# Traced durations in the plan of a list scheduler: the matmul costs, the score products and the lag of a DMA landing

## The chip, the cores and the metric

The kernel runs on one core of a Trainium2 chip, as one program. The metric is the device time of one execution in microseconds; a smaller one is better. A core has TensorE (PE), VectorE (DVE), ScalarE (ACT), GpSimd (POOL) and SyncE (SP), each with a queue of its own that it works off in order; SP's queue issues all DMA transfers here.

## The reference

A decoder trunk of two layers on x (1 × 256 × 1024, float32), conditioned by a vector c. Each layer is a SwiGLU FFN at half weight, a token mixer, and a second SwiGLU FFN at half weight. The mixer of layer 0 is stick-breaking attention (16 heads of 64), that of layer 1 a Griffin RG-LRU block (1280 channels). Before every sub-layer stands an RMSNorm with scale and shift, and behind it a gate; shift, scale and gate come from c.

```python
def sublayer_input(x, g, mod_j):
    shift, scale, gate = mod_j[:, 0], mod_j[:, 1], mod_j[:, 2]
    h = rmsnorm(x, g) * (1 + scale[:, None, :]) + shift[:, None, :]
    return h, (1 + gate)[:, None, :]

for layer in range(DEPTH):
    mod = (c_act @ mod_w[layer] + mod_b[layer]).reshape(B, N_SUB, 3, D_MODEL)
    h, g = sublayer_input(x, norm_g[layer, 0], mod[:, 0])
    x = x + MACARON_W * g * swiglu(h, ffn_w_gu[layer, 0], ffn_w_down[layer, 0])
    h, g = sublayer_input(x, norm_g[layer, 1], mod[:, 1])
    ...  # y: attention (layer 0) or RG-LRU (layer 1) of h
    x = x + g * y
    h, g = sublayer_input(x, norm_g[layer, 2], mod[:, 2])
    x = x + MACARON_W * g * swiglu(h, ffn_w_gu[layer, 1], ffn_w_down[layer, 1])
return rmsnorm(x, final_norm_g)
```

The feed-forward width is 2816. All weights are float32, some 250 MB with the 2 × 9216 × 1024 modulation matrix, and each is read once.

## The kernel before

**Data.** x stays on the chip, transposed: eight tiles x[d] of 128 channels by 256 tokens. A product in float32 accuracy is made of three faster ones: each weight tile of 128 × 2048 (1 MB, a ring `raw` of three) is split by ScalarE into a high half `wh` (L497) and by VectorE into the rest `wl` (L500), 1024 columns at a time, in rings of seven each. Activations are split in the same way. One group (`Acc.group`, L526) is three matmuls on one PSUM bank: wh·xh, wh·xl, wl·xh, each of 256 columns. `group32` (L543) is one matmul in four passes.

**Stages, in order of time.** FFN(0,0), attention(0,1), FFN(0,2), FFN(1,0), RG-LRU(1,1), FFN(1,2), and a last norm. An FFN goes over 22 up tiles (`up`, then `swiglu_tile`) and 11 down tiles of 256 rows (`down`). Attention goes over eight pairs of heads (called heads 0 to 7 here): projection, `scores` (masked start, 12 products at L912, softplus on ScalarE, L923 and the split L740 on VectorE), `sums` (running sums, exponent, split), `values` (L959, then the split L967); the projection of V goes in four parts between them, and the last stage is `down` with the eight tiles of `wo`.

**Boundaries.** `down` leaves the last rows of the last two tiles for the end and finishes the column tiles in the order (0,1), (2,3), (4,5), 6, 7. As each is done, `residual` adds it to x[d] (L666), `add_square` adds x[d]² to a running sum (L601), and `scaled` makes from x[d] and the next scale the first inputs of the next stage, with two more columns for the shift (L623 to L626, so 258 columns). `up_first` lets TensorE work on the first two weight tiles with these inputs that are not normalised yet. Between the two it forms the sum over partitions (`rstd`, L608), and the result is multiplied by rstd afterwards. For the other weight tiles `norm_chunk` (L634 to L636) makes normalised inputs.

**Modulation.** Shift, scale and gate of a sub-layer are 24 multiplies of a 128 × 1024 tile with silu(c), each with its sum: `mod_tile`, a load of 512 KB into a ring `rawm` of three, and one VectorE instruction with an accumulator (L564). Eight of them and one `mod_final` (L568 to L585; the shift's is L577) make one vector. The first two vectors are made at the start; the other 16 wait in a list, `todo`, in the order

```python
    parts = [(0, 0, 2), (0, 1, 1), (0, 1, 0), (0, 1, 2), (0, 2, 1), (0, 2, 0), (0, 2, 2)]
    parts += [(1, i, w) for i in range(3) for w in (1, 0, 2)]
```

(layer, sub-layer, 0 shift, 1 scale, 2 gate), and `hook` puts them into the program at some 1.3 to 1.5 for each weight tile. "Multiplies" below are counted over all 144, the first sixteen included; 49 to 64 are the scale and the shift of FFN(0,2).

**What sets the order.** The function `trunk` does not emit instructions. It describes operations to `Program.op`, each with its engine, a cost in ns and what it reads and writes. `Program.schedule` then runs a list schedule over all five engines, and each queue is emitted in the order of the planned starts. An operation of TensorE has a due time, the sum of the costs of the TensorE operations described before it (`nominal`). Going backwards, every other operation gets its due time from its users: their due time less its cost and less a lag (`LAT`) that depends on its engine. At each step an engine takes, of the operations that could start within 60 ns of the first, the one with the earliest due time; VectorE and ScalarE may wait for a more urgent one (`wait_for`). So the planned times of TensorE and of the landings decide which work VectorE, ScalarE and SP put first, and in places the order of TensorE. The planned times have no part in the execution: there, queues and semaphores alone hold.

Costs in the plan: a VectorE instruction 68 + 1.042 n ns, a ScalarE one 93 + 0.83 n, a DMA by its bytes; the matmuls' cost and the lags are the lines that change. The load of a `mod_tile` waits in the plan for the last TensorE operation described before it (`after=[pr.last_pe]`).

Of the kernel before, what the change touches and what calls it, by code (L numbers as in the profile page):

```python
# [15 lines left out]
T = 256  # L16
# [81 lines left out]
                 "start", "end", "seq", "soft", "lat")  # L98


LAT = {"PE": 230.0, "ACT": 210.0, "DVE": 170.0, "DMA": 2000.0, "POOL": 200.0}
START = {"PE": 1170.0, "DVE": 2840.0, "ACT": 1960.0, "DMA": 1750.0}
SAME = {"PE": 0.0, "ACT": 140.0, "DVE": 60.0, "DMA": 0.0, "POOL": 100.0}

# [1 line left out]
class Program:  # L106
# [53 lines left out]
    def lag(a, b, data):  # L160
        if a.eng == b.eng:
            return SAME[a.eng] if data else 0.0
        return (a.lat or LAT[a.eng]) if data else 100.0

    def schedule(self):
# [30 lines left out]
        for o in ops:  # L196
            o.left, o.ready = len(o.deps), 0.0
        free = {e: START.get(e, 0.0) for e in LAT}
        cand = {e: [] for e in LAT}
        for o in ops:  # L200
# [153 lines left out]


def c_mm(n, passes=3):
    return passes * (max(n, 256) / 2.4 + 2.5)


def c_dma(n):  # L360
# [4 lines left out]
def trunk(ctx, tc, xT, cb, par, modw, gu0, gu, wdn, qk, wv, wo, win, wri, wout, out):  # L365
# [3 lines left out]
    pr = Program()  # L369
# [104 lines left out]
    def A(o, i, f, n, r, w, table=None, psum=False, ptr=0, after=(), **kw):  # L474
        def fn():
            act.activation(o(), i(), f, **{k: (v() if callable(v) else v) for k, v in kw.items()})  # L476
        return pr.op("ACT", c_act(n, psum, ptr), fn, r, w, after, table)

    def V(fn, n, r, w, cost=None, ptr=0):
        return pr.op("DVE", cost or c_dve(n) + 62.0 * ptr, fn, r, w)  # L480
# [26 lines left out]
    class Acc:  # L507
# [6 lines left out]
        def group(self, part, o, w, wc, xs, xc, stop, parts=(None,), passes=(0, 1, 2)):  # L514

            b = self.b
            start = not self.started
            self.started = True
            wh, wl = w
            xh, xl = xs  # L520

            def fn():
                seq = ((wh, xh), (wh, xl), (wl, xh))
                for n, i in enumerate(passes):
                    u, v = seq[i]
                    pe.matmul(o(b()), wc(u()), xc(v()), start=start and n == 0, stop=stop and n == len(passes) - 1,  # L526
                              skip_group_check=True)

            n = xs_n[0]
            rd = [wh, wl] + [(t, q) for t in (xh, xl) for q in parts]  # L530
            if not start:
                rd.append((b, "start"))
            wr = [(b, part)] + ([(b, "start")] if start else [])
            return pr.op("PE", c_mm(n, len(passes)), fn, rd, wr)
# [3 lines left out]
    def group32(acc, part, o, w, wc, x32, xc, n, stop):  # L538

        b = acc.b  # L540
        start = not acc.started
        acc.started = True
        pr.op("PE", c_mm(n, 4), lambda: pe.matmul(o(b()), wc(w()), xc(x32()), start=start, stop=stop, skip_group_check=True),  # L543
              [w, x32] + ([] if start else [(b, "start")]), [(b, part)] + ([(b, "start")] if start else []))
# [58 lines left out]
    def rstd(gen):  # L603
        qs = ssq.pop(gen)
        qs = qs if isinstance(qs, tuple) else (qs,)
        b = Buf(banks)
        for i, q in enumerate(qs):
            pr.op("PE", c_mm(T, 4), lambda i=i, q=q: pe.matmul(b()[:, :T], ones, q(), start=i == 0, stop=i == len(qs) - 1),  # L608
                  [q] + [b] * (i > 0), [b])
        r = Buf(rmsr)  # L610
        o = Buf(rstr)
        A(r, lambda: b()[:, :T], AF.Ln, T, [b], [r], table="lnexp", psum=True, ptr=1, bias=eps_t, scale=1.0 / D)
        A(o, r, AF.Exp, T, [r], [o], table="lnexp", scale=-0.5)
        return o
# [123 lines left out]
    def split(y, a, n):  # L738
        A(y[0], a, AF.Copy, n, [a], [y[0]])
        V(lambda: dve.tensor_tensor(y[1](), a(), f32(y[0]()), ALU.subtract), n, [a, y[0]], [y[1]])  # L740
# [66 lines left out]
    def attention(l, s, nxt, hook):  # L807
# [78 lines left out]
        def hd(ap, e):  # L886
            return ap[:, e * S : (e + 1) * S]

        def scores(f):

            qh, ql = qs.pop(f)
            zs[f] = Buf(banks), Buf(banks)
            u = Buf(F, 6, name=f"u{f}")

            def masked(e):
                b = zs[f][e]

                def fn():
                    diag = b().rearrange("p (e t) -> p e t", e=2)[:, :, :P]
                    pe.matmul(diag, ident, mask.rearrange("p (e t) -> p e t", e=2), start=True, stop=False,  # L900
                              skip_group_check=True)
                pr.op("PE", c_mm(T, 1), fn, [], [b])

            zb = zs[f]

            def products():

                for i, (kc, qc) in enumerate(((slice(T, T + P), slice(0, T)), (slice(T + P, 2 * T), slice(P, T)))):
                    for n, (v, w) in enumerate(((qh, qh), (qh, ql), (ql, qh))):
                        for e in range(2):  # L910
                            rows = slice(e * 64, (e + 1) * 64)
                            pe.matmul(zb[e]()[:, BL[i]], v()[rows, kc], w()[rows, qc], start=False,  # L912
                                      stop=i == 1 and n == 2, skip_group_check=True)

            for e in range(2):
                masked(e)
            pr.op("PE", 2 * c_mm(T), products, [qh, ql], list(zb))
            for e in range(2):
                A(lambda e=e: hd(u(), e), lambda b=zs[f][e]: b()[:, :S], AF.Abs, S, [zs[f][e]], [(u, e)], psum=True)
            A(u, u, AF.Exp, W2, [u], [u], table="lnexp", scale=-1.0)  # L920
            A(u, u, AF.Ln, W2, [u], [u], table="lnexp", bias=1.0)
            for e in range(2):
                V(lambda e=e, b=zs[f][e]: dve.scalar_tensor_tensor(hd(u(), e), b()[:, :S], 0.0, hd(u(), e), ALU.max, ALU.add),  # L923
                  S, [zs[f][e], (u, e)], [(u, e)])
            y = ws_[f] = Buf(R, 6, name=f"sh{f}"), Buf(R, 6, name=f"sl{f}")
            split(y, u, W2)
# [49 lines left out]
        for f in range(8):  # L976
            hook(f)
            q_proj(f)
            if f >= 2:
                values(f - 2)  # L980
            if f in (0, 1, 3, 5):
                v_proj((f + 1) // 2)
            if f >= 1:
                sums(f - 1)
            scores(f)
# [289 lines left out]
```

## Time and profile before

| | |
|---|---|
| runs of the kernel | 997.62, 997.88, 999.67 us; median 997.88 |
| profiled execution | 996.92 us, its span 994.8 us, so 2.1 us lie around the span |
| granted TensorE clock | 0.996 of full speed (mean) |
| TensorE | 976.2 us busy (98%), 8096 instructions |
| VectorE | 799.0 us (80%), 1316 instructions |
| ScalarE | 562.3 us (57%), 902 instructions |
| DMA | 251.24 MB, 253 GB/s over the span |
| weight splits on VectorE (L500) | 328, 390.0 us |
| modulation multiplies (L564) | 144, 174.5 us |

The stages in the trace: FFN(0,0) to about 188 us, attention with `wo` to 321, FFN(0,2) to about 505, FFN(1,0), the RG-LRU block and FFN(1,2) to the end. A row of a group, "L500 DVE TENSOR_TENSOR wl<-raw,wh", gives the line, the engine, the operation and output<-inputs. A duration of one instruction contains a start that overlaps the instruction before it, so two of the same kind can start closer together than a duration. "hx" are inputs of a matmul, "arenar" and "arenaf" the phase's large tiles (split activations, scores), "mf" a finished modulation vector.

### The profile page before, as it was taken

What the parts mean: (1) busy time and instruction counts of PE and PEld (TensorE: products, weight loads), DVE (VectorE), ACT (ScalarE), POOL (GpSimd) and SP (SyncE); (2) the same over time, 40 slices, a digit from 0 to 9 for tenths busy, and PEclk for the clock granted to TensorE, in tenths of its full rate; (3) what the DMA queues carried; (4) which work ended last, traced back from release to release, by engine and by line L of the source; (5) the groups of instructions that cost most, each with busy time, mean ns of one, the idle gap of its engine ahead of it and who ended that gap; (6) DMA issues with size and microseconds to landing.
All of it is one profiled execution on the core that took longest, in us unless ns stands there. A gap on an engine that the chain in (4) does not pass through costs nothing.

```text
span 994.8 us, 19695 instructions
## 1 busy us (share of the span) xinstructions
PE 976.2 (98%) x8096; PEld 964.5 (97%) x8096; DVE 799.0 (80%) x1316; ACT 562.3 (57%) x902; POOL 2.2 (0%) x14
## 2 busy tenths in 40 slices
PE   6999999999999999999999999999999999999997
PEld 5999999999999899999999999999999999999996
DVE  7997888798888999888789988874997996555433
ACT  5475453478785754445366544443779785444333
POOL 0000000000000000000000000000000000000000
PEclk9999999999999999999999999999999999999999
DMA  8988899835556499889866888985244645555431
GB/s 332 352 325 315 331 333 330 334 136 203 198 206 236 170 341 336 331 327 341 326 246 253 329 327 333 343 324 212 108 134 164 254 175 209 204 175 186 166 115 43
DMA packets 48331, 251.24 MB, mean 253 GB/s; under 512 B 5489, under 2 KB 6129, under 8 KB 28530
## 3 DMA queue, kind: packets, MB, share of 16 engines
q1 hardware_dynamic: 48242, 249.99, 68.5%
q8 instruction: 63, 1.03, 0.4%
q14 instruction: 26, 0.21, 0.1%
HBM read 248.92 MB, written 1.05 MB: 251 GB/s over the span
## 4 chain that ended last, share of the span: by engine, by line
PE 95%; DVE 2%; DMA 1%; issue 0%; ACT 0%; SPq 0%; DVEq 0%
PE bank L526 89%; PE bank L836 2%; PE bank L1033 1%; PE bank L959 1%; DVE rawm L564 1%; PE bank L543 1%; PE bank L912 1%; PE bank L937 1%; DMA rawm<-in_modw 1%; DMA x<-in_xT 0%; PE bank L608 0%; PE bank L939 0%; DVE ssq L601 0%; DVE wl L500 0%; DVE x L666 0%
## 5 line engine op out<-in xcount | busy, mean ns | idle before, releaser
L526 PE MATMUL bank<-hx,wh 128*128 128x256 f32 (+1 forms) x3392 | 610.2, 283 | 5.1 <-ACT hx L476 4.8
L526 PEld LDWEIGHTS bank<-hx,wh 128*128 128x128 f32 x3392 | 522.3, 189 | 8.2 <-ACT hx L476 5.7
L497 ACT ACTIVATE wh<-raw 128x1024 fp32r<-128x1024 f32 (+1 forms) x328 | 336.8, 1046 | 340.1 <-PE bank L526 228.6
L500 DVE TENSOR_TENSOR wl<-raw,wh 128x1024 fp32r<-128x1024 f32 (+1 forms) x328 | 390.0, 1210 | 133.2 <-ACT wh L497 130.0
L526 PE MATMUL bank<-hx,wl 128*128 128x256 f32 (+1 forms) x1696 | 476.3, 281 | 0.0
L526 PEld LDWEIGHTS bank<-hx,wl 128*128 128x128 f32 x1696 | 321.2, 189 | 0.3 <-DVE wl L500 0.3
L526 PE MATMUL bank<-arenar,wh 128*128 128x256 f32 x1664 | 294.3, 280 | 0.0
L526 PEld LDWEIGHTS bank<-arenar,wh 128*128 128x128 f32 x1664 | 254.0, 188 | 0.1
L526 PE MATMUL bank<-arenar,wl 128*128 128x256 f32 x832 | 232.5, 279 | 0.0
L564 DVE SCALAR_TENSOR_TENSOR rawm<-rawm,cact 128x1024 f32<-128x1024 f32 x144 | 174.5, 1220 | 10.2 <-DMA rawm<-in_modw 10.0
L526 PEld LDWEIGHTS bank<-arenar,wl 128*128 128x128 f32 x832 | 156.3, 188 | 0.0
L476 ACT ACTIVATE arenar<-a 128x256 fp32r<-128x256 f32 x88 | 35.2, 404 | 4.9 <-DVE a L735 4.8
L740 DVE TENSOR_TENSOR arenar<-a,arenar 128x256 fp32r<-128x256 f32 x88 | 36.4, 419 | 0.5 <-ACT arenar L476 0.5
L735 DVE TENSOR_TENSOR a<-bank,sg 128x256 f32<-128x256 f32 x82 | 34.2, 419 | 0.1
L476 ACT ACTIVATE sg<-bank 128x256 f32<-128x256 f32 x82 | 30.2, 368 | 5.2 <-PE bank L526 1.7
L666 DVE SCALAR_TENSOR_TENSOR x<-bank,mf,x 128x256 f32<-128x256 f32 x48 | 22.1, 480 | 11.8 <-PE bank L526 11.6
L476 ACT ACTIVATE hx<-hpre,mf 128x256 fp32r<-128x256 f32 x48 | 23.2, 503 | 13.6 <-DVE mf L577 6.6
L476 ACT ACTIVATE hx<-x,mf 128x256 fp32r<-128x256 f32 x40 | 19.3, 504 | 20.3 <-DVE x L666 20.2
L636 DVE SCALAR_TENSOR_TENSOR hx<-hpre,mf,hx 128x256 fp32r<-128x256 f32 x48 | 22.8, 482 | 1.3 <-ACT hx L476 1.3
L634 DVE SCALAR_TENSOR_TENSOR hpre<-x,mf,rst 128x256 f32<-128x256 f32 x48 | 21.9, 482 | 2.3 <-ACT rst L476 1.9
L836 PE MATMUL bank<-wh,hx 128*128 128x256 f32 x128 | 23.7, 283 | 0.0
L476 ACT ACTIVATE arenaf<-arenaf 128x768 f32<-128x768 f32 (+1 forms) x31 | 21.9, 735 | 0.3
(97 smaller groups left out, 452.6 us busy)
## 6 DMA issues: line engine op xcount, KB each, us to landing
raw<-in_gu SPq DMA_DIRECT2D x79, 1024.0 KB, 4.9
rawm<-in_modw SPq DMA_DIRECT2D x144, 512.0 KB, 5.9
raw<-in_wdn SPq DMA_DIRECT2D x44, 1024.0 KB, 5.0
raw<-in_win SPq DMA_DIRECT2D x10, 1024.0 KB, 4.7
raw<-in_qk SPq DMA_DIRECT2D x8, 1024.0 KB, 4.8
raw<-in_gu SPq DMA_DIRECT2D x14, 512.0 KB, 6.7
raw<-in_wout SPq DMA_DIRECT2D x5, 1024.0 KB, 5.0
raw<-in_wv SPq DMA_DIRECT2D x4, 1024.0 KB, 4.7
```

Source lines behind the costliest of these rows:

```text
L476: act.activation(o(), i(), f, **{k: (v() if callable(v) else v) for k, v in kw.items()})
L497: act.activation(h()[:, :m], raw()[:, a : a + m], AF.Copy)
L500: dve.tensor_tensor(lo()[:, :m], raw()[:, a : a + m], f32(h()[:, :m]), ALU.subtract)
L526: pe.matmul(o(b()), wc(u()), xc(v()), start=start and n == 0, stop=stop and n == len(passes) - 1, skip_group_check=True)
L543: pr.op("PE", c_mm(n, 4), lambda: pe.matmul(o(b()), wc(w()), xc(x32()), start=start, stop=stop, skip_group_check=True), [w, x32] + ([] if ...
L564: dve.scalar_tensor_tensor(raw(), raw(), 1.0, cact(), ALU.mult, ALU.mult, accum_out=m()[:, t : t + 1])
L634: V(lambda: dve.scalar_tensor_tensor(hp(), x[d](), gs()[:, c], q(), ALU.mult, ALU.mult), T, [x[d], (gs, d), q], [hp], ptr=1)
L636: V(lambda: dve.scalar_tensor_tensor(lo()[:, :T], hp(), sh()[:, c], f32(hi()[:, :T]), ALU.add, ALU.subtract), T, [hp, (sh, d), hi], [lo], ...
L666: dve.scalar_tensor_tensor(x[d](), acc.b()[:, j * T : (j + 1) * T], gate()[:, d : d + 1], x[d](), ALU.mult, ALU.add)
L735: V(lambda: dve.tensor_tensor(a(), b()[:, T:], sg(), ALU.mult), T, [(b, (1, 0)), sg], [a])
L740: V(lambda: dve.tensor_tensor(y[1](), a(), f32(y[0]()), ALU.subtract), n, [a, y[0]], [y[1]])
L836: pe.matmul(o, u()[:, tb * P : (tb + 1) * P], v()[:, c0 : c0 + 256], start=start and n == 0, stop=k == KD - 1 and n == 2, skip_group_check ...
```

## The change

Three numbers of the plan change; the operations described to it stay the same. The lag from a DMA's end to its landing goes from 2000 to 3500 ns. A matmul group is planned at 117.8 ns for each pass of 256 columns (109.2 before; 353.4 ns for a group instead of 327.5), a four-pass one at 432 (436.7 before), in proportion to the columns above 256. The 12 score products of a head are planned at 730 ns (655 before). `c_mm` also stands in the costs of `sums`, `values`, the V projection and `rstd`, and the sum of all of them sets the due times of everything.

```diff
-LAT = {"PE": 230.0, "ACT": 210.0, "DVE": 170.0, "DMA": 2000.0, "POOL": 200.0}
+LAT = {"PE": 230.0, "ACT": 210.0, "DVE": 170.0, "DMA": 3500.0, "POOL": 200.0}
...
 def c_mm(n, passes=3):
-    return passes * (max(n, 256) / 2.4 + 2.5)
+    return (432.0 if passes == 4 else 117.8 * passes) * max(n, 256) / 256
...
             for e in range(2):
                 masked(e)
-            pr.op("PE", 2 * c_mm(T), products, [qh, ql], list(zb))
+            pr.op("PE", 730.0, products, [qh, ql], list(zb))
```

## The prediction

> **What bounds the kernel now.** I read the page's busy times first, then the chain, then what TensorE waits for, then windows around each wait.
>
> ```profile
> span 994.8 us, 19695 instructions
> PE 976.2 (98%) x8096; PEld 964.5 (97%) x8096; DVE 799.0 (80%) x1316; ACT 562.3 (57%) x902; POOL 2.2 (0%) x14
> PE 95%; DVE 2%; DMA 1%; issue 0%; ACT 0%; SPq 0%; DVEq 0%
> ```
>
> TensorE is busy in 98% of the span and is 95% of the chain. A new order of the same operations can only win what TensorE loses: 994.8 − 976.2 = 18.6 us, the start and the end among it, and matmuls run at a low clock. Where else it loses, its waits tell:
>
> ```profile
> PE bank L526 <- ACT hx L476: 4.8, 2, 2.5
> PE bank L608 <- DVE ssq L601: 0.9, 1, 0.9
> ```
>
> ```profile
> 323.60 0.61 PE L526 MATMUL bank<-hx,wh 128*128 128x258 f32 x2 [2.22 <-ACT hx L476]
> ...
> 329.48 0.39 PE L526 MATMUL bank<-hx,wh 128*128 128x258 f32 x1 [0.27 <-DVE hx L624]
> ...
> 332.94 0.70 PE L608 MATMUL bank<-ssq,ones 128*128 128x256 f32 x2 [0.94 <-DVE ssq L601]
> ```
>
> The bracket is the idle time before a matmul and its releaser. Of the 4.8 us, the longer wait, 2.5, is at the start of the kernel; the 2.22 us before 323.60, and the two smaller gaps after it, lie at one place: the boundary from attention to the second FFN of layer 0. TensorE has ended `wo`'s products and wants the scaled inputs (`scaled`, L623 to L626), then the sum of squares (L601 into L608). Windows there, TensorE alone (start:end, length, busy and matmuls, granted clock, DMA share, GB/s):
>
> ```profile
> 321.40:323.60 2.20, 0.00 (x0) 1.00 0.82 266
> 323.60:327.80 4.20, 4.20 (x21) 0.60 0.80 253
> 327.80:333.00 5.20, 3.99 (x30) 1.00 0.46 181
> 342.00:346.00 4.00, 3.92 (x29) 1.00 0.61 248
> ```
>
> The idle is followed by 4.20 us at a granted clock of 0.60. The boundary thus costs 2.22 + 0.27 + 0.94 = 3.43 us of idle and 4.20 × (1 − 0.60) = 1.68 us of slow clock: 5.1 us. Why the inputs are late stands in the chain of waits:
>
> ```profile
> 313.58 5.50 DMA rawm<-in_modw
> 319.08 0.02 issue
> 319.10 2.47 DVE rawm L564 x4
> 321.57 0.40 DVE hx L626
> 321.96 1.16 DVE rawm L564 x2
> 323.12 0.02 issue
> 323.14 0.17 DVE mf L577
> ```
>
> The last multiplies of the adaLN shift (L564, `mod_tile`) stand in VectorE's queue between the residuals; `mod_final` (L577) makes the shift only at 323.14, and no `scaled` input exists without it. How many such multiplies, and how full VectorE is:
>
> ```profile
> L564 DVE SCALAR_TENSOR_TENSOR rawm<-rawm,cact x9: 1218/1220/1226, 302.5 to 321.9; 128x1024 f32<-128x1024 f32 x9
> ...
> 310.00:333.00 23.00, 19.57 (x150) 18.79 (x148) 22.44 (x52) 13.05 (x30) 0.00 (x0) 0.93 0.69 246
> ```
>
> (The second row is a window with every engine: PE, PEld, DVE, ACT, POOL, then clock, DMA share, GB/s.) Nine multiplies stand within 20 us, and VectorE is busy 22.44 of 23.00 us. Here VectorE sets the end, and nowhere else after the start does an engine other than TensorE.
>
> **The change part by part.** It removes and adds no operation; I count in the orders that the two planners emit, which need no time. A multiply costs VectorE the distance of two starts, 1.15 us:
>
> ```profile
> 313.46 1.22 DVE L564 SCALAR_TENSOR_TENSOR rawm<-rawm,cact 128x1024 f32<-128x1024 f32 x1
> ...
> 314.61 1.22 DVE L564 SCALAR_TENSOR_TENSOR rawm<-rawm,cact 128x1024 f32<-128x1024 f32 x1
> ```
>
> *The costs themselves.* The old plan gives a matmul of 256 columns 256/2.4 + 2.5 = 109.2 ns, the new one 117.8. The trace, in a stretch without a gap:
>
> ```profile
> 360.00:500.00 140.00, 140.00 (x1191) 140.00 (x1190) 120.68 (x189) 65.10 (x97) 0.00 (x0) 1.00 0.90 332
> ```
>
> 140.00 us / 1191 = 117.5 ns, so the new plan is right and the old one ran TensorE 7.5% too fast. The Trainium skill ("TensorE: Matmul & The Clock Gate", Part 1, "Wait — 56ns, not 53.3ns?") gives N/2.4 GHz + about 2.5 ns between warm matmuls, which is the old cost to the digit and speaks against this edit; by it that stretch would have held 1282 matmuls. The measured row decides. In a plan with a slower TensorE, VectorE gets through more of its queue per weight tile, so multiplies and their loads, which only wait for a place behind a TensorE operation, are emitted further ahead. The longer lag of a DMA asks for loads 1.5 us sooner.
>
> *Multiplies moved ahead.* Finished multiplies at the same weight split of VectorE's queue, old to new: at FFN 0's last up tile 26 to 30; at head 0's projection 45 to 51; at head 4's second half 48 to 55; at `wo`'s first tile, second half, 51 to 61; at `wo`'s last tile 58 to 63; at the second FFN's first tile 64 to 66. The boundary needs 64 (FFN 2's scale and shift are multiplies 49 to 64). The old order does 56 to 64 inside 302 to 323 us. The new one has done 64, and L577 behind them, before the second half of `wo`'s last tile is split; two multiplies of the gate, which the boundary doesn't need, stay there. So some seven multiplies, 7 × 1.15 = 8.1 us of VectorE, leave the 20 us in front of the boundary.
>
> *What is late next there.* The column tiles of `down` end in the order (0,1), (2,3), (4,5), 6, 7. TensorE ends at 321.4. Per d VectorE has L666 0.40, L624 0.07, L626 0.40 and L601 0.33 (chain pieces):
>
> ```profile
> 327.43 0.40 DVE x L666
> 327.83 0.07 DVE hx L624
> 327.89 0.33 DVE ssq L601
> ...
> 329.42 0.40 DVE hx L626
> ```
>
> that is 1.2 us, and 9.6 for eight; the five weight splits of this window are 5.8 more. One d feeds six matmuls, 0.7 us, so d = 7 is wanted at 321.4 + 7 × 0.7 = 326.3, the sum at 321.4 + 48 × 0.1175 = 327.0. The last residual can start at 321.6 and be through by 323; even with two weight splits before it (2.3 us) it is in time by 1 us. So the idle goes, and with it the slow clock: −5.1 us. The bounds: 0, and −5.9 from the other end of the same stretch (from 321.38 to 332.94, 11.56 us, less 48 × 0.1175 = 5.64).
>
> *Behind the boundary.* In the new order four weight splits (4.6 us) stand among the first normalised chunks (L634 to L636), at about 333 to 336. The old order loses little there: 4.00 − 3.92 = 0.08 us of idle in 342 to 346, 29 matmuls instead of 34. I put 0 on it, bounds −0.6 to +1.0.
>
> *Attention, where the multiplies go.* These windows carry every engine:
>
> ```profile
> 205.00:243.00 38.00, 38.00 (x325) 37.09 (x325) 33.10 (x61) 31.01 (x55) 0.00 (x0) 1.00 0.44 154
> 243.00:276.00 33.00, 33.00 (x275) 32.06 (x274) 28.20 (x42) 26.36 (x43) 0.00 (x0) 1.00 0.62 223
> 276.00:297.00 21.00, 21.00 (x180) 19.95 (x179) 18.33 (x29) 18.31 (x33) 0.00 (x0) 1.00 0.51 181
> ```
>
> From 205 to 243 both orders do none or one (33.10 + 1.15 of 38). From 243 to 276 the old one does 3 (48 to 51), the new one 7 (54 or 55 to 61): 28.20 + 4 × 1.15 = 32.8 of 33.00 us. From 276 to 297 it does 1 instead of 4: 18.33 − 3.45 = 14.9 of 21.00. So one window gets full, between two with room of 3.8 and 6.1 us. What waits behind a multiply is the softmax's VectorE part (L923, L740), and behind it TensorE's `sums` and `values` of that head. If every idle moment of VectorE in that window is a wait for ScalarE that the multiplies can't fill, VectorE falls behind by 4.6 us and TensorE with it; if they fill them, nothing. TensorE has no idle in any of the three rows, so some slack exists; I take a quarter, +1.2 us, the point where the TensorE order itself changes (v0's second half before head 0's scores, 12 products planned at 730 instead of 655 ns) among it. Both ends, 0 and +4.6, stay for the range.
>
> *Everything else.* From 325 to 505 us eight more multiplies and loads. At 332 GB/s for a share of 0.90 a load of 0.524 MB takes 1.42 us of the DMA engines: 11 us in 180, share 0.90 to 0.96. Such a share is seen with TensorE full:
>
> ```profile
> 14.00:60.00 46.00, 46.00 (x373) 45.63 (x373) 45.48 (x87) 24.50 (x34) 0.00 (x0) 1.00 0.97 359
> ```
>
> VectorE has 140 − 120.68 = 19 us free in 140. SP's queue is in order, and a multiply's load put ahead of a weight load holds it until one of three `rawm` cells is free. The cover is the ring of seven split halves, each 8 groups of three matmuls, 24 × 0.1175 = 2.8 us of TensorE's work; I cost it at nothing, at most 1 us between 60 and 100 us, where the first loads swap. Past the multiplies (after 670 us) the orders differ little: 0.
>
> Sum: −5.1 + 1.2 + 0 = −3.9 us. The profiled execution, 996.92 us (span 994.8 and 2.1 around it), would be 993.0; it lies 1.0 below the median of the runs, 997.88, from which the forecast is **994.0 us**.
>
> **The rivals.** About 0.2%, 2 us, is what a measurement of this kernel can tell from no change.
>
> *A: given back in attention.* VectorE's idle from 243 to 276 is mostly fixed, so 3 to 4.6 us of the 5.1 come back as gaps before `sums` and `values`: −2.1 to −0.5, about 996.6. For it: ScalarE is busy 26.36 of 33 there and VectorE's softmax steps wait for it. Against: no TensorE gap at all there now.
>
> *B: slower.* The same late VectorE makes TensorE wait 2.2 us or more in one piece at two heads, and each is followed by the slow clock as at 323.60: 2 × (2.2 + 1.7) = 7.8 us, less 5.1: +2.7, 1000.6 us. It decides once two waits are that long, which needs 4.4 of the 4.6 us unfilled; the 0.27 us gap at 329.48 shows no clock loss in its row, which is at 1.00. So it is unlikely but priced by rows.
>
> *C: the clock loss is no child of the gap.* The Trainium skill (same page, Part 1, "What's actually happening") lets the clock drop after an idle window of about 3.4 us; by it 2.22 us could pass without a drop. Here a clock of 0.60 stands straight behind 2.20 us of idle, so I don't believe that a drop would stay without one; if it did, the gain would be 3.4 − 1.2 = 2.2 us, 995.7.
>
> *D: it does nothing.* The shift's last multiplies or ScalarE's copies come as late on the chip as before, since loads land when they land: 997.9.
>
> **How the numbers follow.** Forecast 0.55, A 0.20, B 0.14, C 0.05, D 0.06. The forecast's own range is −5.1 to −2.3, with −0.6 from behind the boundary and −0.4, half of what its two ends (5.1 and 5.9) leave: 991.8 at the low end. Upward, A and D are taken in, and B only where one long wait comes instead of two (−5.1 + 3.9 + 1.2 + 1.0 = +1.0, with the median's own spread of 1): 999.6. Left out are most of B and 0.05 below. Faster by over 0.2%: the forecast, a third of A and most of C, 0.65; slower: B and a little of A, 0.16; the rest, 0.19, within.
>
> **What would show it.** Right: no gap over 0.5 us between 321 and 333, granted clock 1.00 there, L577 before the last residuals, and multiplies of FFN 2's shift between 243 and 276. Wrong: L526 or L608 still waiting for hx or ssq; waits of L937, L939 or L959 for arenar between 215 and 300; TensorE waiting for wl or wh (L497, L500), which would say that loads were held back.

## The result and the profile after

The changed kernel takes 992.15 us in the median of four runs (990.72 to 993.6), the kernel before 997.75 (997.33 to 999.67): a ratio of 0.994, 95% interval 0.9921 to 0.996. That is 5.6 us by the medians and 6.0 by the ratio, at the low end of the range. The same kernel measured again (e5) gave a ratio of 0.9943 (0.9931 to 0.9955). The profiled execution took 992.5 us, its span 990.8. Two single runs are left out of the ratios below, one of e14 (3970.83 us) and one of e1 (1184.26 us at a granted clock of 0.755), and the trace of e1, which is of that run, is left out of the table.

From the page of the changed kernel, the lines that answer to those shown of before:

```profile
span 990.8 us, 19720 instructions
PE 975.0 (98%) x8096; PEld 963.2 (97%) x8096; DVE 797.1 (80%) x1316; ACT 561.7 (57%) x902; POOL 2.2 (0%) x14
PE 89%; DMA 5%; DVE 5%; ACT 1%; issue 1%; SPq 0%; DVEq 0%; ACTq 0%
```

The busy times are the same within 2 us: the work is the same, and what went is waiting. TensorE's waits (us in total, times, longest), then windows of TensorE alone around the boundary:

```profile
PE bank L526 <- ACT hx L476: 3.1, 1, 3.1
...
PE bank L526 <- DVE hx L636: 0.4, 2, 0.2
```

```profile
318.00:333.00 15.00, 15.00 (x127) 1.00 0.49 180
333.00:345.00 12.00, 12.00 (x104) 1.00 0.37 130
```

The 3.1 us are at the start; the wait at the boundary is gone, and from 318 to 345 us TensorE has no idle and clock 1.00. Where else the time moved, the same matmul groups tell, by their starts in two traces. I take six of them that stand at the same place of both queues: 44.8 us (the start is over), 297.6 (`wo` begins), 320.9 (`wo`'s last group), 332.9 (L608), 347.2, 529.6 (behind the next boundary), and the last matmul, 987.0. The table gives what each stretch takes more (+) or less than in the trace of before, in us, for this kernel and all that follow:

| kernel | start | to wo | wo | boundary | behind it | to 529.6 | rest | all |
|---|---|---|---|---|---|---|---|---|
| changed | +1.29 | +0.08 | +0.47 | −5.95 | −1.02 | +0.78 | +0.35 | −4.00 |
| e5 changed again | +0.65 | +0.05 | +0.46 | −5.95 | −1.02 | −0.01 | +0.33 | −5.49 |
| e2 DMA lag alone | +0.07 | +0.59 | +0.03 | −0.25 | −0.94 | 0.00 | −0.21 | −0.71 |
| e3 sixteen ahead | +0.61 | +1.80 | +0.15 | −4.43 | −0.93 | 0.00 | 0.00 | −2.80 |
| e4 shift held back | −0.21 | −0.01 | +0.20 | −5.90 | −1.02 | +0.04 | +0.28 | −6.62 |
| e6 matmul cost alone | +1.01 | +0.09 | +0.49 | −5.97 | −1.00 | +4.41 | +0.68 | −0.29 |
| e7 multiplies short | +0.69 | −0.17 | 0.00 | −1.21 | −0.94 | 0.00 | +0.02 | −1.61 |
| e8 six put back | −0.69 | +1.57 | +1.54 | −2.40 | +0.15 | +0.03 | +0.33 | +0.53 |
| e9 and loads short | +0.70 | 0.00 | 0.00 | −1.20 | −0.78 | −0.02 | 0.00 | −1.30 |
| e10 loads short | +0.39 | −0.17 | 0.00 | −0.62 | −0.21 | 0.00 | +1.43 | +0.82 |
| e11 cost, mod lag | +1.36 | 0.00 | +0.48 | −5.96 | −1.01 | +1.49 | +0.56 | −3.08 |
| e12 plan too slow | −0.13 | +9.87 | +0.45 | −5.97 | −0.02 | +6.42 | +1.41 | +12.03 |
| e13 splits later | +0.42 | −0.01 | 0.00 | +0.07 | +0.87 | +0.01 | −0.01 | +1.35 |
| e14 and multiplies | +0.38 | −0.17 | 0.00 | −1.59 | +0.52 | 0.00 | +0.01 | −0.85 |
| e15 and loads too | +0.51 | −0.18 | 0.00 | −4.14 | +0.50 | 0.00 | +0.01 | −3.30 |
| e16 half way | +1.12 | +0.56 | +0.26 | −5.96 | −1.01 | −0.02 | +0.48 | −4.57 |

The whole gain lies at the boundary and just behind it, 6.97 us; the rest gives back 1 to 3. The start's column is not the change's: kernels with the old order there lie between +0.07 and +0.70 (e2, e3, e7, e9, e10, e13 to e15), those with the new order between −0.69 and +1.36, and the same kernel twice at +1.29 and +0.65. The column "to wo" is not free of such differences either: e8 has the order of the changed kernel up to 309 us and yet loses 1.5 us more there, from a gap of 0.82 us at the boundary in front of attention (208.13 us) on.

What the kernel before loses behind the boundary shows little in TensorE's own waits. It stands in the rows of its weight loads (PEld, from 333 to 348 us), which wait for normalised inputs (L636) and for a split (L500); the changed kernel has no such wait there:

```profile
PEld bank L526 <- DVE hx L636: 0.4, 2, 0.2
PEld bank L526 <- DVE wl L500: 0.3, 1, 0.3
```

Attention, where the forecast saw the price, in windows with every engine (changed kernel; PE, PEld, DVE, ACT, POOL, then clock, DMA share, GB/s):

```profile
205.00:243.00 38.00, 38.00 (x325) 37.00 (x325) 33.66 (x63) 32.58 (x57) 0.00 (x0) 1.00 0.44 146
243.00:276.00 33.00, 33.00 (x275) 32.01 (x275) 32.06 (x49) 26.50 (x43) 0.00 (x0) 1.00 0.73 256
276.00:297.00 21.00, 21.00 (x176) 19.97 (x175) 18.89 (x30) 18.95 (x32) 0.00 (x0) 1.00 0.71 249
```

VectorE went from 28.20 to 32.06 us of 33.00, and TensorE still has no idle: the multiplies filled gaps of VectorE. (Six multiplies start from 243 to 276 us and three from 276 to 297; the prediction counted seven and one.)

### The profile page after: what moved, and what is told of

Read it like the earlier page. It is cut to its first block, busy times and chain, and to the rows that moved or that the text cites. A ratio compares the mean times of both kernels' runs of the same rounds, so it can differ in the third digit from the quotient of the medians.

```text
span 990.8 us, 19720 instructions
## 1 busy us (share of the span) xinstructions
PE 975.0 (98%) x8096; PEld 963.2 (97%) x8096; DVE 797.1 (80%) x1316; ACT 561.7 (57%) x902; POOL 2.2 (0%) x14
## 4 chain that ended last, share of the span: by engine, by line
PE 89%; DMA 5%; DVE 5%; ACT 1%; issue 1%; SPq 0%; DVEq 0%; ACTq 0%
PE bank L526 82%; DMA rawm<-in_modw 2%; PE bank L836 2%; DVE wl L500 2%; DMA raw<-in_gu 1%; PE bank L1033 1%; PE bank L959 1%; PE bank L543 1%; PE bank L912 1%; DMA x<-in_xT 1%; DVE rawm L564 1%; PE bank L937 1%; DVE hx L636 1%; DVE hpre L634 0%; ACT wh L497 0%
## 5 line engine op out<-in xcount | busy, mean ns | idle before, releaser
L500 DVE TENSOR_TENSOR wl<-raw,wh 128x1024 fp32r<-128x1024 f32 (+1 forms) x328 | 389.4, 1210 | 128.6 <-ACT wh L497 126.5
L740 DVE TENSOR_TENSOR arenar<-a,arenar 128x256 fp32r<-128x256 f32 x88 | 36.6, 421 | 1.2 <-ACT arenar L476 1.2
L636 DVE SCALAR_TENSOR_TENSOR hx<-hpre,mf,hx 128x256 fp32r<-128x256 f32 x48 | 22.8, 480 | 0.1
```

What stands on the lines that cost most here:

```text
L500: dve.tensor_tensor(lo()[:, :m], raw()[:, a : a + m], f32(h()[:, :m]), ALU.subtract)
L636: V(lambda: dve.scalar_tensor_tensor(lo()[:, :T], hp(), sh()[:, c], f32(hi()[:, :T]), ALU.add, ALU.subtract), T, [hp, (sh, d), hi], [lo], ...
```

## The experiments

### One part of the change alone

**e1 and e6: the matmul cost alone**

```diff
-    return passes * (max(n, 256) / 2.4 + 2.5)
+    return (432.0 if passes == 4 else 117.8 * passes) * max(n, 256) / 256
```

> The matmul cost alone (117.8 ns a pass, 432 for four passes; the score products follow it at 706.8 ns, the DMA lag stays at 2000). In its planned order 64 multiplies are done before the second half of wo's last tile, as in the changed kernel. Theory (the multiplies' move ahead of the boundary is the gain): no gap over 0.5 us and clock 1.00 from 321 to 333 us, 990.5 to 993.5 us, within 1 us of the changed kernel. Rival (the earlier loads from the longer DMA lag carry a good part): at least 2 us of the gain is missing, 994 us or more.

> The matmul cost alone once more, since the granted clock was 0.755 in the profile of its first look and its times spread from 994 to 1002 us. Theory (the matmul cost moves the multiplies, and that is the gain): 990 to 993.5 us, no gap and clock 1.00 from 321 to 333 us. Rival (the DMA lag is needed too): 995 us or more, with waits for wl, wh or hx that the changed kernel doesn't have.

Measured: e1 997.64 us (1.0005, 0.9989 to 1.0021), e6 997.73 us (1.0016, 0.9995 to 1.0036). The trace read here is e6's. The single runs of both scatter widely, e6's from 990.97 to 1003.48 us; why is open. There is no gain, so the theory missed twice and the rivals' times came. But in the trace the first boundary wins 6.97 us in full, and the next one (505 to 530 us) loses 4.41. VectorE there and TensorE's window behind its gap:

```profile
508.22 1.23 DVE L564 SCALAR_TENSOR_TENSOR rawm<-rawm,cact 128x1024 f32<-128x1024 f32 x1 [1.35 <-DMA rawm<-in_modw]
```

```profile
513.40:515.10 1.70, 0.00 (x0) 1.00 0.06 27
515.20:519.40 4.20, 3.95 (x19) 0.63 0.35 121
```

VectorE takes its queue in order. It stands 1.35 us before a multiply whose tile has not landed, and the residuals behind it come late. The plan with the old lag gives such a load 1.48 us of transfer and 2.0 of lag; from issue to landing it takes much longer: 6.6 us in the median from 490 to 515 us of e6, and over a whole execution (page of the changed kernel: line, count, KB, median us):

```profile
rawm<-in_modw SPq DMA_DIRECT2D x144, 512.0 KB, 6.3
```

In the changed kernel a landing holds VectorE longer still at this boundary, but ahead of the first residual, which starts at 504.35:

```profile
500.93 1.23 DVE L564 SCALAR_TENSOR_TENSOR rawm<-rawm,cact 128x1024 f32<-128x1024 f32 x1 [2.97 <-DMA rawm<-in_modw]
```

So VectorE still waits for a landing; what differs is that in e6 the wait stands between two residuals (506.00 and 510.16).

**e2: the DMA lag alone** (`"DMA": 2000.0` to `3500.0`)

> The DMA lag of 3500 ns alone, old matmul costs. 658 places of VectorE's queue differ from the kernel before, but the multiplies stand as there: 58 before the second half of wo's last tile, 61 to 64 at the second FFN's first tile. Theory: the gap of 2.2 us and the slow clock are still there, 997 to 999 us. Rival (loads earlier, any reorder helps): 993 to 995.5 us.

Measured: 996.78 us (0.9999, 0.999 to 1.0008). No gain; a gap of 2.71 us stands before the first scaled inputs, with a mean clock of 0.63 behind it. That is what the theory said, and the time is just under its range.

**e11: the matmul cost, and the lag for the multiplies' loads only**

```diff
 (e1's line, and in mod_tile:)
+        lat = lat or 3500.0
         load_ = dma(raw, modw[l, (s * 3 + w) * KD + t], D, [raw], after, lat)
```

> The matmul cost alone, and the lag of 3500 ns for the loads of the multiplies only; weight loads keep 2000. With the matmul cost alone the first boundary won 6.9 us and the next one (505 to 530 us) lost 4.4: VectorE stood in front of multiplies whose loads had not landed, with residuals queued behind. Theory (the lag matters because it keeps a multiply out of the queue until its load is there): both boundaries are clean, 990 to 993 us. Rival (the weight loads' lag is what helps): the second boundary loses 3 us or more again, 995 us or more.

Measured: 990.28 us (0.9943, 0.9932 to 0.9955), as the changed kernel; the second boundary loses 1.49 instead of 4.41 us (the changed kernel: 0.78 and nothing in its two traces). So the matmul cost wins the first boundary, and the lag of the multiplies' loads saves most of the second. Two parts of the change are not needed for the time: the weight loads' lag, and the 730 ns of the score products, which are planned at 706.8 here.

### What holds the boundary

**e3: sixteen multiplies ahead in the old plan** (`o.prio = p - o.early`, with 10 us for the multiplies of FFN 2's scale and shift)

> The kernel before with one edit: the sixteen multiplies of FFN 2's scale and shift get a due time 10 us earlier; all planned durations are the old ones. 129 places of VectorE's queue and 45 of TensorE's differ; all 64 multiplies are done before wo's last-but-one tile, and 9 instead of 3 stand between 243 and 276 us. Theory: the boundary's whole loss goes (traced in the changed kernel: 6.9 us from 319.5 to 347), the start stays as before, 990.5 to 993 us; attention gives back under 1 us. Rival (the new durations matter in many places): 995 us or more. Rival (multiplies in attention stall the softmax): gaps of TensorE between 243 and 276 of 2 us and more in sum.

Measured: 992.03 us (0.9953, 0.9938 to 0.9967). An early due time for the multiplies alone wins 5.4 us at the boundary and behind it (the planner then moves ScalarE's splits back too, see e13), and attention gives back 1.8, where under 1 was expected. First all engines, then TensorE's weight loads from 224 to 300 us:

```profile
243.00:276.00 33.00, 32.81 (x268) 31.23 (x268) 29.14 (x44) 23.85 (x39) 0.00 (x0) 1.00 0.66 229
```

```profile
PEld bank L961 <- DVE arenar L742: 0.7, 2, 0.4
PEld bank L939 <- DVE arenar L742: 0.5, 1, 0.5
```

VectorE does less here than in the changed kernel (29.14 against 32.06 us), and TensorE loses more. So a full VectorE is not what costs TensorE time. The softmax's split (L742, before's L740) comes late, for which neither of the other two kernels makes TensorE wait. That a multiply's place in front of it is the reason is not shown: VectorE itself waits for ScalarE there, 1.07 us at 258.40.

**e4: the shift held back in the changed kernel** (`lat = 25000.0` for the loads of its eight multiplies)

> The changed kernel with one edit: the loads of the eight shift multiplies of FFN 2 are planned to land 25 us late, so that 58 are done at wo's first tile and 61 at its last, as in the kernel before. Theory: a gap of 1.5 to 2.5 us before the first scaled inputs with a clock under 0.8 after it comes back, 996 to 999 us. Rival (the gain comes from other parts of the new order): 991 to 993.5 us.

Measured: 991.01 us (0.9935, 0.9922 to 0.9948). The theory's gap did not come back. Only three multiplies were left behind 306 us, and the shift was ready just in time:

```profile
319.04 1.22 DVE L566 SCALAR_TENSOR_TENSOR rawm<-rawm,cact 128x1024 f32<-128x1024 f32 x1
320.18 0.09 DVE L566 DVE_READ_ACCUMULATOR rawm<-rawm,cact 128x1 f32 x1
320.30 0.17 DVE L579 TENSOR_TENSOR mf<-mr,pars 128x8 f32<-128x8 f32 x1
```

The shift may come at 320.3, so a shift at 300 us, as in the changed kernel, is not needed for the gain; the run was too mild to tell more.

**e8: six idle VectorE instructions put back**

```diff
+            if (l, s, w) == (0, 2, 2) and t in (1, 2):
+                for _ in range(2 * t):
+                    dve.tensor_tensor(raw(), raw(), raw(), ALU.max)
             dve.scalar_tensor_tensor(raw(), raw(), 1.0, cact(), ALU.mult, ALU.mult, accum_out=m()[:, t : t + 1])
```

> The changed kernel, its planned order untouched, with six idle VectorE instructions of 1024 columns (a tile's maximum with itself) added: two before the multiply at 309.5 us and four before the one at 316.6 us, about 6.9 us of VectorE. Theory (VectorE's work in front of the boundary sets it): a gap of 1.5 us or more returns between 319 and 333 us, with a clock under 0.8 behind it, +3 to +6 us on the changed kernel: 994.5 to 998 us. Rival (only the moment of the shift counts, which is 300 us here and stays): under 1 us, 991 to 993 us.

Measured: 997.3 us (1.0007, 0.9998 to 1.0016): the gain is gone, though the shift is ready as early. From `wo` to 347 us it loses 5.8 us more than the changed kernel for 7.5 us of VectorE (by the starts in its trace, 2.52 and 5.02 us), in gaps of 1.21 us and less. The forecast gap with a low clock did not come: the clock stays at 1.00 from 326 to 334. So work of VectorE in front of the boundary is enough to lose the time there.

**e7, e9, e10: the six multiplies 59 to 64 short in the old order, their loads too, the loads alone**

```diff
-            dve.scalar_tensor_tensor(raw(), raw(), 1.0, cact(), ...
+            k = 8 if (l, s, w) == (0, 2, 0) and t >= 2 else D
+            dve.scalar_tensor_tensor(raw()[:, :k], raw()[:, :k], 1.0, cact()[:, :k], ...
 (e9 and e10, for the same tiles:)
+            load_ = pr.op("DMA", c_dma(D), lambda: sp.dma_start(raw()[:, :8], src[:, :8]), ...
```

> The kernel before, its planned order untouched in every queue, but the six shift multiplies 59 to 64 take 8 of their 1024 columns (so their part of the shift is not the reference's), about 1.05 us less of VectorE each, 6.3 us within 313 to 323 us. Theory (VectorE's multiplies in front of the boundary are the whole cause): the gap of 2.2 us, the slow clock and the 0.9 us before L608 go, and what the boundary gains is 5 to 7 us: 990.5 to 992.5 us. Rival (the place of weight splits and residuals in the new order does part of it): at most half, 994.5 us or more.

> The kernel before, planned order untouched, with the six shift multiplies 59 to 64 and their six loads cut to 8 of 1024 columns (so their part of the shift is not the reference's). With the multiplies alone cut, VectorE stood idle 2.72, 1.08 and 0.67 us in front of three of them, for their landings, and TensorE won only 2.2 us between 319 and 347. Theory (two chains end nearly together there, VectorE's work and the landings in a ring of three cells): with both cut the whole boundary goes, -6 to -7 us between 319 and 347, 990 to 992.5 us. Rival (weight splits and residuals in the old order bind as well): -4 us or less, 993.5 us or more.

> The kernel before, planned order untouched, with only the six loads cut to 8 columns; the multiplies keep their 1024 columns on what the cell held (not the reference's shift). Theory of two chains: VectorE's 7 us of multiplies keep the shift late, -0.5 to -3 us between 319 and 347, 994 to 996.5 us. Rival (the landings alone bind): -5 us or more, 990.5 to 992.5 us.

Measured: e7 995.73 us (0.9984, 0.9975 to 0.9993), e9 995.14 (0.9982, 0.9973 to 0.999), e10 996.08 (0.9993, 0.9984 to 1.0002). The boundary wins 1.21, 1.20 and 0.62 of 5.95 us. So taking the multiplies away is not enough, against what the prediction says, and with their loads it isn't either; e7 and e9 came out where their rivals had put them, e10 in its theory's range. In e7 VectorE waits for landings; in e9 no longer, but for ScalarE, and ScalarE for TensorE. First VectorE of e7 and e9, then ScalarE of e9 (the bracket is the idle before):

```profile
319.70 0.17 DVE L565 SCALAR_TENSOR_TENSOR rawm<-rawm,cact 128x8 f32<-128x8 f32 x1 [2.72 <-DMA rawm<-in_modw]
```

```profile
319.48 0.17 DVE L583 TENSOR_TENSOR mf<-mr,pars 128x8 f32<-128x8 f32 x1
319.56 0.48 DVE L672 SCALAR_TENSOR_TENSOR x<-bank,mf,x 128x256 f32<-128x256 f32 x1
323.11 0.16 DVE L630 TENSOR_TENSOR hx<-mf,hx 128x2 fp32r<-128x2 f32 x1 [3.08 <-ACT hx L476]
```

```profile
320.98 2.00 ACT L497 ACTIVATE wh<-raw 128x1024 fp32r<-128x1024 f32 x2 [2.97 <-PE bank L526]
322.89 0.28 ACT L476 ACTIVATE hx<-mf 128x2 fp32r<-128x2 f32 x2
```

The shift is ready at 319.65, but its copies stand in ScalarE's queue behind two weight splits, which wait 2.97 us for a `wh` cell that TensorE frees at the end of `wo`. The same two stand in the profile before, where the copies behind them wait for the shift:

```profile
320.29 2.00 ACT L497 ACTIVATE wh<-raw 128x1024 fp32r<-128x1024 f32 x2 [0.77 <-PE bank L526]
323.35 0.30 ACT L476 ACTIVATE hx<-mf 128x2 fp32r<-128x2 f32 x2 [1.05 <-DVE mf L577]
```

In every kernel above that wins the boundary these two splits stand further back in ScalarE's queue. Counted from the first scaled input, they are 12 and 17 places behind it in the changed kernel and 8 and 19 in e3, against 6 and 7 in the kernel before and 6 and 8 in e2, which wins nothing. ScalarE in the changed kernel, where the first of the two comes after the copies (hx<-x) of six column tiles, and waits for nothing:

```profile
316.36 0.91 ACT L476 ACTIVATE hx<-x,mf 128x256 fp32r<-128x256 f32 x2 [2.32 <-DVE x L666]
...
318.68 0.51 ACT L476 ACTIVATE hx<-x,mf 128x256 fp32r<-128x256 f32 x1 [0.80 <-DVE x L666]
...
319.47 0.51 ACT L476 ACTIVATE hx<-x,mf 128x256 fp32r<-128x256 f32 x1
...
321.32 0.91 ACT L476 ACTIVATE hx<-x,mf 128x256 fp32r<-128x256 f32 x2 [0.65 <-DVE x L666]
322.14 0.71 ACT L476 ACTIVATE sq<-x 128x256 f32<-128x256 f32 x2
322.75 1.05 ACT L497 ACTIVATE wh<-raw 128x1024 fp32r<-128x1024 f32 x1
```

**e13, e14, e15: three of ScalarE's splits moved by hand; with the multiplies short; with their loads too**

```diff
     order = pr.schedule()
+    late = [o for o in order if o.seq in (1777, 1857, 1859)]
+    order = [o for o in order if o not in late]
+    at = next(i for i, o in enumerate(order) if o.seq == 1763) + 1
+    order[at:at] = late
```

> The kernel before with one change in ScalarE's queue only: three weight splits (two at 320.29 us and one at 325.18 us in the profile before) go behind the last square of the boundary; every other queue keeps its order. Theory (three things end nearly together at this boundary: the splits of ScalarE, which wait for a cell that TensorE frees at 321; VectorE's multiplies; the landings): the shift is still made at 323, so TensorE wins 0.5 to 2.5 us between 319 and 347, 994.5 to 996.5 us. Rival (ScalarE's splits alone are the cause): -5 us or more, 990 to 992.5 us.

> The same three splits moved, and the six shift multiplies cut to 8 columns with their loads whole (so their part of the shift is not the reference's). Theory of three: the last landing at 322.2 us still sets the shift, about 1 us of gap is left, -3 to -5 us between 319 and 347, 992 to 994.5 us. Rival (landings never bind once the other two are gone): -6 us or more, 990 to 992 us.

> The same three splits moved, and the six multiplies and their loads cut to 8 columns (so their part of the shift is not the reference's). Theory of three: nothing is left to wait for, no gap over 0.5 us and clock 1.00 from 321 to 333 us, -5.5 to -7 us between 319 and 347, 990 to 992 us. Rival (the order of residuals and weight splits on VectorE binds as a fourth): -4 us or less, 993 us or more.

Measured: e13 998.24 us (1.001, 1.0001 to 1.0019), e14 996.12 (0.9989, 0.998 to 0.9998), e15 993.62 (0.9969, 0.9956 to 0.9981). At the boundary +0.07, −1.59 and −4.14 us: the splits alone win nothing, the splits and the multiplies little, all three together most of it. The three end within 1 us of each other: the last landing at 322.2 us (e7), the copies behind the splits start at 322.9 (e9), the multiplies end at 323.1 (before). So each hides the other two. One pair, splits and loads without the multiplies, was not run.

The theory of three holds in kind, but all three forecasts missed. e13 won nothing, e14 less than said, and e15 came out where its rival is: −3.64 us from 319 to 347 us, so the order on VectorE binds as a fourth. Of the 1.8 us of the 5.95 that e15 leaves, half is idle in front of the sum of squares, whose last addition still stands behind a weight split (L607 is before's L601):

```profile
PE bank L614 <- DVE ssq L607: 0.9, 1, 0.9
PE bank L526 <- DVE hx L630: 0.2, 1, 0.2
```

Behind the boundary e13 to e15 lose 0.5 to 0.9 us, where the changed kernel wins 1.02. TensorE's weight loads wait there for normalised inputs (0.8 to 0.9 us) and for a split (0.2 to 0.3); that the splits moved there cause both is likely, but not shown.

### How exact must the plan be?

**e16 and e12: 113.5 and 125.0 ns instead of 117.8, the rest as changed**

> The changed kernel with 113.5 instead of 117.8 ns a pass, half way between the old and the new plan; the DMA lag stays at 3500. 59 and 61 multiplies are done at wo's last tile, 64 at the second FFN's first tile. Theory (what helps is a plan that knows when TensorE frees a cell, so an error of 3.5% leaves some splits too early): a gain, but under that of the changed kernel, 991.5 to 996 us. Rival (any slower plan does as well as 117.8): 990 to 992 us.

> The changed kernel with 125.0 instead of 117.8 ns a pass, so a plan 6% slower than the trace. Some ten multiplies instead of seven stand between 243 and 276 us and eleven more are done at the first boundary. Theory (VectorE's room in attention, 33 us with 32.06 busy now, is used up): TensorE loses 1 to 4 us between 229 and 300 us, 992.5 to 996 us. Rival (any slower plan does as well): within 1 us of the changed kernel, 990 to 992.5 us.

Measured: e16 991.21 us (0.9942, 0.9929 to 0.9954), e12 1006.77 us (1.0093, 1.0073 to 1.0112). Half way is as good as the traced value, as e16's rival had it. A plan 6% slower than the trace loses 9.87 us up to `wo`, more than was expected, and 6.42 from 347 to 530 us:

```profile
205.00:243.00 38.00, 34.98 (x266) 32.45 (x265) 35.27 (x70) 31.27 (x54) 0.00 (x0) 0.96 0.56 201
```

Most of the 9.87 us, some 7, is lost by 227 us, and not in the softmax but at the boundary in front of attention. Two multiplies stand among the residuals there, where the kernel before has none. VectorE, then TensorE's waits from 200 to 226 us:

```profile
202.82 1.22 DVE L564 SCALAR_TENSOR_TENSOR rawm<-rawm,cact 128x1024 f32<-128x1024 f32 x1
```

```profile
PE bank L526 <- DVE hx L626: 1.4, 2, 1.2
PE bank L836 <- DVE hx L636: 1.2, 3, 0.5
```

A stretch of slow clock follows (last section). Waits for the softmax's split (L740) come later, 1.2 us from 226 to 300 us. So the stall that rival B priced exists only in small, and not at the 117.8 of the change. A slower plan helps, but not any.

**e5: the changed kernel again** (no edit)

> The changed kernel as it is, beside the others of this job. Its first profile began the steady part 1.3 us later than the kernel before (first groups of TensorE, 0 to 45 us) and spent 0.1 us more in attention. If the 1.3 us are the jitter of the first transfers, this profile's start differs from it by more than 0.5 us and the runs lie between 989.5 and 993.5 us; if they come from the four swapped places of VectorE's queue before 20 us, the start is again 1.1 to 1.5 us later than in the kernel before.

Measured: 991.2 us (0.9943), the start 0.64 us earlier than in its first profile: jitter.

## Why the prediction was right and wrong

- **The bound and the place: right.** Only TensorE's losses could be won, and they were, where forecast. No gap, clock 1.00, the shift ahead of the last residuals: all as said.
- **The sum: three terms mis-sized, all to the same side.** Taken were −5.1 (boundary), 0 (behind it) and +1.2 (attention), −3.9 in all. Measured were −5.95, −1.02, and +0.08 up to `wo` or +0.55 with it. The start and the rest gave back some of that, and 5.6 to 6.0 us are left in the runs.
- **The boundary's term counted idle and slow clock.** Its other reckoning, by the starts of matmuls over the stretch, gave 5.9, was kept as a bound, and was right. An idle time is counted from the modelled end of a matmul, here 0.28 us behind its start, while matmuls otherwise start every 0.1175 us (two rows of the kernel before):

```profile
331.72 0.28 PE L526 MATMUL bank<-hx,wl 128*128 128x258 f32 x1
332.94 0.70 PE L608 MATMUL bank<-ssq,ones 128*128 128x256 f32 x2 [0.94 <-DVE ssq L601]
```

From start to start this gap costs 1.22 − 0.12 = 1.10 us, not 0.94. The three gaps cost 3.92 us in this way instead of 3.43, the start after each is late by 0.1 to 0.2 more, and with the 1.7 us of slow clock the sum is 6.0.
- **The boundary's cause was wrong.** The step that failed is "VectorE sets the end": I read the chain of waits, which shows only the one that came last, and never ScalarE's queue. e7 to e15 put three in its place (VectorE's multiplies, their landings in a ring of three, two splits of ScalarE that wait for TensorE), and a fourth, the sum of squares. Shortening the six multiplies alone (e7) wins only 1.21 of the 5.95 us. That the direction came out is partly luck: the new order also moves the splits, which the prediction never counted.
- **Behind the boundary:** I counted TensorE's idle (0.08 us) and gave the missing matmuls (29 instead of 34 in 4 us) a place in the bound only. From 333 to 345 us it is 94 against 104, by waits of the weight loads.
- **Attention was priced too high.** VectorE's 32.8 us of 33.00 was forecast well (32.06); that a full VectorE must hold TensorE was not so. Rival A fell with it.
- **The matmul cost and the lag.** "Loads 1.5 us sooner" was said of the lag and no price given; e6 and e11 show that it is worth 2.9 us at the second boundary.
- **The range** ended at 991.8 us, where the measured ratio lies. Its low end took half of what the boundary's two reckonings differ by, and −0.6 behind it; measured were the whole and −1.02.
- **Rival C** is not borne out: in the changed kernel no slow stretch stayed at the boundary. e12 shows that one can come without a long gap (last section). **D** fell.

## What to carry to other kernels

Where one wait is followed back, look at what else stands in every in-order queue at that moment: with three chains ending together, taking one away won at most a fifth of the whole. In a list schedule, give the bottleneck engine its traced time: here a plan 3.7% short did as well, one 7% short put refills in front of urgent steps, and one 6% long put filler there. Give a load a landing near the traced one, above all where the instruction that waits for it stands ahead of other work. Price a gap by the starts of the matmuls around it, and read the weight loads' waits beside TensorE's own. An order's effect can be tested by moving three instructions or by shortening six in the finished order, without a new plan.

## What the runs showed of the hardware

An idle TensorE of 2.22 (before), 2.30 (e13) and 2.71 us (e2) was followed by 4.1 to 4.2 us at a mean clock of 0.58 to 0.63. One of 1.77 us was too (0.63, e6), but not one of 1.61 (e10) or 1.75 us (e12). These are windows of e13 and of e12:

```profile
321.80:324.00 2.20, 0.00 (x0) 1.00 0.96 264
324.10:328.20 4.10, 4.10 (x20) 0.58 0.86 271
```

```profile
523.60:525.30 1.70, 0.02 (x1) 1.00 0.05 19
525.40:530.00 4.60, 3.28 (x22) 1.00 0.31 114
```

These means depend on where the window is cut. In the clock's record in the traces of the table the value is 1.00 or 0.50, and each slow stretch inside a kernel lasts 3.41 us. In the kernel before it begins at 324.44 us, 0.8 us after the idle has ended:

```profile
321.00:324.40 3.40, 1.18 (x9) 1.00 0.80 241
324.50:327.80 3.30, 3.30 (x17) 0.50 0.78 248
```

In e12 one begins at 221.24 us, though no idle in the 10 us before it is longer than 0.53 us; but TensorE was busy only 2.23 of the 3.40 us in front of it:

```profile
217.80:221.20 3.40, 2.23 (x12) 1.00 0.71 299
221.30:224.60 3.30, 3.24 (x15) 0.50 0.00 0
```

In each of the five traces with such a stretch (before, e2, e6, e12, e13) it begins a whole number of 3.413 us ahead of the slow stretch at the kernel's end; in the kernel before, 324.44 and 990.03 us are 195 of them apart. So these stretches begin on a fixed grid, and several short waits can bring one on. A limit can't be given: from 521.6 to 525.0 us of e12 TensorE was busy 1.82 of 3.40 us, and no slow stretch followed.

The Trainium skill ("TensorE: Matmul & The Clock Gate", Part 1, "What's actually happening") names an idle window of about 3.4 us that runs freely. The traces agree with its length and with the grid, but the slow stretches came after less idle than a whole window.
